# Rotary embedding on one core: the cosine and sine tables are loaded ahead of the first batch of x

## The chip, the cores and the metric

The kernel runs on one core of a Trainium2 chip. The metric is the device time of one execution in microseconds (us). Before the change the median of 3 runs was 161.33 us, the lowest 161.15 and the highest 161.42.

A core has five engines that run their own instruction streams and meet only at semaphores: TensorE (PE, matmul), VectorE (DVE), ScalarE (ACT), GpSimd (POOL) and SyncE (SP). Transfers between the chip's main memory (DRAM) and the on-chip memory are issued by an engine as an instruction and carried out by 16 DMA engines that all issuers share. In this kernel SyncE and ScalarE issue them, and each has a queue of its own in the profile: q1 is SyncE's, q10 ScalarE's.

## The reference

```python
batch, seq, dim = 16, 512, 1024          # float32, num_heads = 16
x = x.reshape(batch, seq, 16, 64)
x1, x2 = x[..., :32], x[..., 32:]
cos, sin = cos[None, :, None, :], sin[None, :, None, :]      # both (512, 32)
out = np.concatenate([x1 * cos - x2 * sin, x1 * sin + x2 * cos], axis=-1)
```

So every row of x, of 1024 elements, is cut into 16 heads of two halves, and each element becomes itself times cos, plus its partner in the other half times sin, with a minus sign for the first half. x and the output have 33.55 MB each; cos and sin have 64 KB each.

## The kernel before, in words

**Tiles.** The 512 positions of a batch are spread over 128 partitions. The first two and the last two batches are tiles of their own ("singles"): a partition holds 4 positions (R1 = 4), 16 KB of one batch, and the tile is 2 MB. The twelve batches between them are taken in pairs: a partition holds 8 positions (R2 = 8), the tile is 4 MB. That makes 10 tiles, t = 0 to 9, with 4, 4, 8, 8, 8, 8, 8, 8, 4, 4 rows; a "row" u (0 to 63) is 128 partitions by 1024 elements, and it is the unit of compute. The tiles live in a ring of 40 rows in on-chip memory (`x_sb`), and the result of a row overwrites the row.

**One row.** POOL (L257) makes t2 = partner times sin; VectorE (L293) makes t1 = x times cos in PSUM. Then they are added, in one of two ways: VectorE adds them (L304), or, in three of every eight rows (the list PE2), TensorE adds t2 on top of t1 by a matmul with the identity (L224) and ScalarE copies the sum back (L191). In one row of each pair tile VectorE makes t2 as well (L286). A store takes the tile when its last row is done.

**The tables.** cos and sin are loaded in the layout of the single tiles into `stage`, one half each. VectorE copies cos into PSUM (L264) and then waits for the PSUM banks that TensorE clears (L201). ScalarE waits for sin and makes the signed sin table of the single tiles from it (L182 and L183); POOL's first row waits for that table (L251) and then for its tile (L255). For the pair tiles, whose rows lie differently over the partitions, two pairs of matmul instructions (L208) spread both tables into PSUM with a selection matrix (`pick`, which ScalarE makes at L177), and ScalarE makes the second sin table (L186, L187). POOL asks for that one before the first row of tile 2 (L253), VectorE at the same place (L269).

**Order of the transfers.** All loads are issued by ScalarE, in the function `on_scalar`, through the helper at L153. At the start it issues six: tile 0, then cos and sin (L174), then tiles 1 to 5, which fill the ring. The other four loads wait for ring space: tiles 6, 7 and the two singles 8 and 9 are issued after the stores of the first, second and third group of eight ring rows have landed (L194). All stores are issued by SyncE in tile order (L161), each after the adds of its tile; SyncE does nothing before the first of them, and it waits for the last stores at the end (L162). The two queues are independent, so loads and stores share the DMA engines whenever both have work.

Of the kernel before, what the change touches and what calls it, by code (L numbers as in the profile page):

```python
# [6 lines left out]
def bass_split_heads_rope_kernel(  # L7
# [21 lines left out]
    R1 = seq // P  # L29
# [38 lines left out]
    with ExitStack() as stack:  # L68
        x_sb = stack.enter_context(nc.sbuf_tensor([P, RING, H, 2, HALF], fp32))
        t2_sb = stack.enter_context(nc.sbuf_tensor([P, NT2, H, 2, HALF], fp32))  # L70
        stage = stack.enter_context(nc.sbuf_tensor([P, 2, R1 * HALF], fp32))
# [11 lines left out]
        sem_cos = stack.enter_context(nc.semaphore("cos"))  # L83
        sem_sin = stack.enter_context(nc.semaphore("sin"))
# [28 lines left out]
        def in_dram(single, pairs, t):  # L113
            b, n = tiles[t]
            return single[b] if n == R1 else pairs[:, b:b + 2, :]

        def in_sbuf(t):
            b, n = tiles[t]
            k = b * R1 % RING
            return x_sb[:, k:k + n].rearrange("p n h t d -> p (n h t d)")  # L120

        def where(u):
            t, r = rows[u]
            return t, r, u % RING
# [7 lines left out]
        def wait_added(eng, u):  # L132

            if n_pe[u]:
                eng.wait_ge(sem_a, n_pe[u])
            if n_comb[u]:
                eng.wait_ge(sem_v, n_comb[u])
# [10 lines left out]
        def stores_of(k):  # L148

            return sum(b * R1 // R2 == k for b, _ in tiles)  # L150

        def load(eng, t):
            eng.dma_start(in_sbuf(t), in_dram(x1, x2, t)).then_inc(sem_in[t], 16)  # L153

        def on_sync(sp):
            for u in range(NU):
                t, r, k = where(u)
                if r == tiles[t][1] - 1:
                    wait_added(sp, u)
                    k = u // R2  # L160
                    sp.dma_start(in_dram(o1, o2, t), in_sbuf(t)).then_inc(sem_out[k] if k < EARLY else sem_rest, 16)  # L161
            sp.wait_ge(sem_rest, 16 * sum(stores_of(k) for k in range(EARLY, NU // R2)))  # L162

        def on_scalar(ae):
            later = {}
            for t, (b, n) in enumerate(tiles):
                if b * R1 + n <= RING:
                    load(ae, t)
                else:

                    later.setdefault((b * R1 - RING) // R2 * R2 + R2 - 1 + LAG, []).append(t)
                if t == 0:
                    for i, (table, sem) in enumerate(((cos, sem_cos), (sin, sem_sin))):
                        ae.dma_start(stage[:, i, :], table.rearrange("(s r) d -> s (r d)", r=R1)).then_inc(sem, 16)  # L174

            ae.wait_ge(sem_i, 2)
            ae.activation(  # L177
                pick[:], ident[:].rearrange("q (s k) -> q k s", k=2)[:, :, :, None].broadcast_to([P, 2, P // 2, 2]), COPY
            ).then_inc(sem_g, 1)
            ae.wait_ge(sem_sin, 16)  # L180
            sv = stage[:, 1, :].rearrange("s (r d) -> s r d", d=HALF)
            ae.activation(s1_sb[:, :, 0, :], sv, COPY, scale=-1.0)  # L182
            ae.activation(s1_sb[:, :, 1, :], sv, COPY).then_inc(sem_s, 1)  # L183
            ae.wait_ge(sem_t, 2)
            s2 = s2_sb[:].rearrange("p (k r) t d -> p k r t d", r=R1)
            ae.activation(s2[:, :, :, 0, :], pair_ps[:, :, 1, :, :], COPY, scale=-1.0)  # L186
            ae.activation(s2[:, :, :, 1, :], pair_ps[:, :, 1, :, :], COPY).then_inc(sem_s, 1)  # L187
            for u in range(NU):
                if PE2[u]:
                    ae.wait_ge(sem_e, n_pe[u])  # L190
                    ae.activation(xs[:, u % RING, :], t1_ps[:, u % NT1, :], COPY).then_inc(sem_a, 1)  # L191
                for t in later.get(u, ()):
                    k = (tiles[t][0] * R1 - RING) // R2
                    ae.wait_ge(sem_out[k], 16 * stores_of(k))  # L194
                    load(ae, t)
# [65 lines left out]
        def on_vector(ve):  # L261
# [49 lines left out]
            for u in range(NU + LEAD):  # L311
                if u < NU:
                    mul(u)
                if u >= LEAD and not PE2[u - LEAD]:
                    comb(u - LEAD)

        on_sync(nc.sync)
        on_scalar(nc.scalar)
        on_gpsimd(nc.gpsimd)
        on_tensor(nc.tensor)  # L320
# [34 lines left out]
```

## Time and profile before

| What | Value |
|---|---|
| median of 3 runs (lowest to highest) | 161.33 us (161.15 to 161.42) |
| the profiled execution, first to last instruction (its span) | 160.3 us |
| busy: POOL, VectorE, TensorE, ScalarE | 134.9, 130.3, 72.8, 24.4 us |
| bytes moved, mean rate over the span | 67.26 MB, 419 GB/s |
| tables landed and used: VectorE's copy of cos, ScalarE's first use of sin | 9.04 us, 9.26 us |
| POOL's first row begins | 9.85 us |
| first store issued | 20.48 us |
| last tile's first row begins on POOL | 141.02 us |
| last row's add ends on VectorE | 151.63 us |

The profile is of one execution. For that execution only the span is given; the runs are timed from outside it and the median is 1.0 us longer than the span, so a sum made on the span is carried over to the median by adding that difference. Times in the text are counted from the start of the span. A slice table divides the span into 40 parts, with the busy share of each engine in tenths. The chain of waits goes back from the last instruction to what released it, step by step. Besides these views the trace holds a record of every DMA packet: queue, start, duration and size. It doesn't say which of the 16 engines carried a packet.

### The profile page before, as it was taken

The numbers are of one execution on the slowest core, as the hardware profiler recorded it, in microseconds if no ns is written. First come the engines' busy times: TensorE is split into PE (matmuls) and PEld (weight loads), VectorE is DVE, ScalarE is ACT, GpSimd is POOL, SyncE is SP. The second block draws the span as 40 slices with busy tenths as digits, with TensorE's granted clock in tenths as the row PEclk, the third lists the DMA queues.
The fourth block names the chain that finished last, engine by engine and source line by source line (L and its number), as shares of the span: only waits on it lengthen the run. The fifth ranks groups of instructions, "written<-read, shape, count | busy, mean of one in ns | idle before, by whom it ended". The sixth has DMA issues, their size and how long they took to land.

```text
span 160.3 us, 522 instructions
## 1 busy us (share of the span) xinstructions
PE 72.8 (45%) x94; PEld 24.0 (15%) x94; DVE 130.3 (81%) x117; ACT 24.4 (15%) x27; POOL 134.9 (84%) x64
## 2 busy tenths in 40 slices
PE   6050004478357936660847105489458435850000
PEld 1020002022202211210221002022202111220000
DVE  0069998599989999996999709899889999999500
ACT  0420000203120222022012010201220402040000
POOL 1059999999999999999999999699999999289400
PEclk9955555557755587689687965555555977699555
DMA  5999999999999999999999999999999999999896
GB/s 147 409 441 474 409 450 409 425 429 429 446 429 458 417 411 466 409 433 401 450 433 425 425 409 458 409 433 433 411 429 462 441 417 401 450 441 441 376 450 294
DMA packets 3170, 67.26 MB, mean 419 GB/s; under 512 B 352, under 2 KB 608, under 8 KB 608
## 3 DMA queue, kind: packets, MB, share of 16 engines
q10 hardware_dynamic: 1728, 33.69, 49.6%
q1 hardware_dynamic: 1440, 33.56, 48.9%
q14 instruction: 2, 0.02, 0.0%
HBM read 33.69 MB, written 33.55 MB: 419 GB/s over the span
## 4 chain that ended last, share of the span: by engine, by line
DMA 60%; POOL 13%; DVE 8%; PE 7%; issue 3%; ACT 2%; ACTq 1%; DVEq 0%
DMA x_sb<-in_x_dram 41%; DMA out_dram<-x_sb 18%; POOL t_sb L257 13%; PE t_ps L224 7%; DVE t_ps L293 5%; DVE x_sb L304 3%; ACT x_sb L191 2%; ACTq L153 1%; ACTq L174 1%; DVE t_sb L286 0%; DVEq L303 0%
## 5 line engine op out<-in xcount | busy, mean ns | idle before, releaser
L257 POOL TENSOR_TENSOR t_sb<-x_sb,s_sb 128x1024 f32<-128x1024 f32 x58 | 134.2, 2346 | 14.8 <-ACT s_sb L183 8.5
L224 PE MATMUL t_ps<-t_sb,ident 128*128 128x512 f32 x84 | 68.0, 957 | 63.0 <-DVE t_ps L293 39.2
L293 DVE TENSOR_TENSOR t_ps<-x_sb,pair_ps 128x1024 f32<-128x1024 f32 x48 | 57.7, 1223 | 9.9 <-ACT x_sb L191 9.8
L304 DVE TENSOR_TENSOR x_sb<-t_ps,t_sb 128x1024 f32<-128x1024 f32 x43 | 52.4, 1218 | 2.6 <-POOL t_sb L257 2.6
L224 PEld LDWEIGHTS t_ps<-t_sb,ident 128*128 128x128 f32 x84 | 22.1, 290 | 108.9 <-DVE t_ps L293 74.6
L191 ACT ACTIVATE x_sb<-t_ps 128x1024 f32<-128x1024 f32 x21 | 21.5, 1023 | 109.9 <-PE t_ps L224 96.9
L293 DVE TENSOR_TENSOR t_ps<-x_sb,tab_ps 128x1024 f32<-128x1024 f32 x16 | 19.3, 1222 | 0.1
L286 DVE TENSOR_TENSOR t_sb<-x_sb,tab_ps 128x1024 f32<-128x1024 f32 x6 | 7.3, 1213 | 0.0
L264 DVE COPY tab_ps<-stage 128x128 f32<-128x128 f32 x1 | 0.3, 294 | 7.8 <-DMA stage<-in_cos_dram 7.8
L208 PE MATMUL pair_ps<-stage,pick 128*128 128x256 f32 x4 | 2.0, 667 | 5.4 <-DMA stage<-in_sin_dram 5.4
L201 PE MATMUL t_ps<-zero 128*128 128x512 bf16 x6 | 2.7, 627 | 1.3 <-DVE zero L262 1.3
L208 PEld LDWEIGHTS pair_ps<-stage,pick 128*128 128x128 f32 x4 | 1.2, 324 | 6.4 <-issue 6.3
L177 ACT ACT_TABLE_LOAD x1 | 1.3, 1283 | 5.5 <-issue 5.5
L201 PEld LDWEIGHTS t_ps<-zero 128*128 128x128 bf16 x6 | 0.7, 136 | 2.4 <-DVE zero L262 1.2
L262 DVE MEMSET zero<- 128x256 uint32 x1 | 0.3, 272 | 0.9 <-PEq L337 0.9
L186 ACT ACTIVATE s_sb<-pair_ps 128x256 f32<-128x256 f32 x1 | 0.4, 383 | 1.7 <-PE pair_ps L208 1.7
L182 ACT ACTIVATE s_sb<-stage 128x128 f32<-128x128 f32 x1 | 0.3, 309 | 2.1 <-DMA stage<-in_sin_dram 2.1
L235 POOL MEMSET ident<- 128x128 f32 x1 | 0.2, 204 | 0.3 <-POOLq L337 0.3
L177 ACT ACTIVATE pick<-ident 128x256 f32<-128x256 f32 x1 | 0.4, 416 | 0.0
L187 ACT ACTIVATE s_sb<-pair_ps 128x256 f32<-128x256 f32 x1 | 0.4, 379 | 0.0
L237 POOL TENSOR_SCALAR_AFFINE_SELECT ident<-ident 128x128 f32<-128x128 f32 x1 | 0.3, 292 | 0.1
L337 POOL MEMSET const-float32-0.0<- 128x1 f32 x1 | 0.1, 98 | 0.3 <-issue 0.3
(6 smaller groups left out, 1.0 us busy)
## 6 DMA issues: line engine op xcount, KB each, us to landing
x_sb<-in_x_dram ACTq DMA_DIRECT2D x6, 4096.0 KB, 38.0
out_dram<-x_sb SPq DMA_DIRECT2D x6, 4096.0 KB, 25.0
x_sb<-in_x_dram ACTq DMA_DIRECT2D x4, 2048.0 KB, 22.6
out_dram<-x_sb SPq DMA_DIRECT2D x4, 2048.0 KB, 15.2
stage<-in_cos_dram ACTq DMA_DIRECT2D x1, 64.0 KB, 7.8
stage<-in_sin_dram ACTq DMA_DIRECT2D x1, 64.0 KB, 7.5
```

The source lines that it names most:

```text
L153: eng.dma_start(in_sbuf(t), in_dram(x1, x2, t)).then_inc(sem_in[t], 16)
L174: ae.dma_start(stage[:, i, :], table.rearrange("(s r) d -> s (r d)", r=R1)).then_inc(sem, 16)
L177: ae.activation(pick[:], ident[:].rearrange("q (s k) -> q k s", k=2)[:, :, :, None].broadcast_to([P, 2, P // 2, 2]), COPY).then_inc(sem_g, 1)
L186: ae.activation(s2[:, :, :, 0, :], pair_ps[:, :, 1, :, :], COPY, scale=-1.0)
L191: ae.activation(xs[:, u % RING, :], t1_ps[:, u % NT1, :], COPY).then_inc(sem_a, 1)
L201: pe.matmul(t1_ps[:, k, b * BANK:(b + 1) * BANK], zero[:, 0:P], zero[:], start=True, stop=True).then_inc(sem_w, 1)
L208: pe.matmul(pair_ps[:, k].rearrange("p c r d -> p (c r d)"), pick[:, k].rearrange("q s b -> q (s b)"), stage[:].rearrange("q c f -> q (c f)"),
L224: ins = pe.matmul(t1_ps[:, u % NT1, b * BANK:(b + 1) * BANK], ident[:], t2[:, b * BANK:(b + 1) * BANK], start=False, stop=True, skip_group ...
L257: pl.tensor_tensor(t2_sb[:, u % NT2, :, :, :], swapped(k), over_heads(s_of(t, r)), mult).then_inc(sem_p, 1)
L286: ve.tensor_tensor(t2_sb[:, u % NT2, :, :, :], swapped(k), over_heads(v_ps), mult)
L293: ve.tensor_tensor(t1_ps[:, u % NT1, :].rearrange("p (h d) -> p h d", d=HALF), x_sb[:, k, :, :, :].rearrange("p h t d -> p (h t) d"), c_of ...
L304: ve.tensor_tensor(xs[:, k, :], t1_ps[:, u % NT1, :], t2_sb[:, u % NT2, :, :, :].rearrange("p h t d -> p (h t d)"), add,).then_inc(sem_v, 1)
```

## The change

SyncE's first act becomes the load of cos, ScalarE's first act the load of sin. The load of tile 0 follows as ScalarE's second transfer, and the loads of tiles 1 to 5 follow it directly. Destinations, sizes, semaphores and everything that waits for the tables are as before.

```diff
+        def load_table(eng, i, table, sem):
+            eng.dma_start(stage[:, i, :], table.rearrange("(s r) d -> s (r d)", r=R1)).then_inc(sem, 16)
+
         def on_sync(sp):
+            load_table(sp, 0, cos, sem_cos)
             for u in range(NU):
                 t, r, k = where(u)
                 if r == tiles[t][1] - 1:
...
         def on_scalar(ae):
+            load_table(ae, 1, sin, sem_sin)
             later = {}
             for t, (b, n) in enumerate(tiles):
                 if b * R1 + n <= RING:
...
                     later.setdefault((b * R1 - RING) // R2 * R2 + R2 - 1 + LAG, []).append(t)
-                if t == 0:
-                    for i, (table, sem) in enumerate(((cos, sem_cos), (sin, sem_sin))):
-                        ae.dma_start(stage[:, i, :], table.rearrange("(s r) d -> s (r d)", r=R1)).then_inc(sem, 16)
```

## The prediction

> **What bounds the kernel now.** I read the slice table first: it shows whether any resource is full all the time.
>
> ```profile
> span 160.3 us, 522 instructions
> ...
> PE 72.8 (45%) x94; PEld 24.0 (15%) x94; DVE 130.3 (81%) x117; ACT 24.4 (15%) x27; POOL 134.9 (84%) x64
> ...
> DMA  5999999999999999999999999999999999999896
> ...
> q10 hardware_dynamic: 1728, 33.69, 49.6%
> q1 hardware_dynamic: 1440, 33.56, 48.9%
> ```
>
> The DMA row has a 9 in nearly every slice, and the queues' packets fill 49.6 + 48.9 = 98.5% of the span. POOL is at 84%. The DMA engines are the bound, and only the first slice and the last ones have room. So I cut the edges finer (columns: stretch, length, busy PE, PEld, DVE, ACT, POOL, PE clock, DMA share, GB/s):
>
> ```profile
> 2.25:3.50 1.25, 1.25 (x5) 0.29 (x2) 0.00 (x0) 0.00 (x0) 0.00 (x0) 1.00 0.69 210
> 4.00:7.50 3.50, 0.00 (x0) 0.00 (x0) 0.00 (x0) 1.70 (x2) 0.00 (x0) 1.00 0.99 421
> 7.50:8.00 0.50, 0.00 (x0) 0.00 (x0) 0.00 (x0) 0.00 (x0) 0.00 (x0) 0.68 0.84 295
> 8.00:20.00 12.00, 2.05 (x4) 1.18 (x4) 10.35 (x10) 1.17 (x4) 10.15 (x5) 0.50 1.02 438
> 55.00:105.00 50.00, 23.91 (x32) 7.64 (x31) 42.74 (x38) 8.19 (x8) 48.22 (x22) 0.74 1.00 429
> 140.00:158.00 18.00, 2.36 (x5) 0.88 (x4) 10.55 (x10) 2.05 (x2) 9.27 (x4) 0.69 0.99 428
> ```
>
> The rate is about 430 GB/s with loads alone (8 to 20), with both (55 to 105) and with stores alone (140 to 158): the mix does not matter. Below it lie the ramp, up to 4 us, and the dip from 7.5 to 8.0, where the tables' 512-byte packets pass.
>
> Then the start and the end in order of time (start, duration, what):
>
> ```profile
> 0.81 0.37 ACTq L153 DMA_DIRECT2D x_sb<-in_x_dram  x1
> 1.21 0.46 ACTq L174 DMA_DIRECT2D stage<-in_cos_dram  x1
> 1.69 0.45 ACTq L174 DMA_DIRECT2D stage<-in_sin_dram  x1
> 2.17 3.27 ACTq L153 DMA_DIRECT2D x_sb<-in_x_dram  x5
> 9.04 0.29 DVE L264 COPY tab_ps<-stage 128x128 f32<-128x128 f32 x1 [7.84 <-DMA stage<-in_cos_dram]
> 9.26 0.31 ACT L182 ACTIVATE s_sb<-stage 128x128 f32<-128x128 f32 x1 [2.08 <-DMA stage<-in_sin_dram]
> 9.85 32.35 POOL L257 TENSOR_TENSOR t_sb<-x_sb,s_sb 128x1024 f32<-128x1024 f32 x14 [8.48 <-ACT s_sb L183]
> ...
> 135.58 16.46 SPq L161 DMA_DIRECT2D out_dram<-x_sb  x3
> 141.02 9.27 POOL L257 TENSOR_TENSOR t_sb<-x_sb,s_sb 128x1024 f32<-128x1024 f32 x4 [3.92 <-DMA x_sb<-in_x_dram]
> 150.40 1.23 DVE L304 TENSOR_TENSOR x_sb<-t_ps,t_sb 128x1024 f32<-128x1024 f32 x1 [1.08 <-POOL t_sb L257]
> ```
>
> Tile 0 lands at about 8.8 (issued at 0.81, shortest landing 8.0), but POOL starts at 9.85, because it waits for the sin table. At the end POOL waits for the last load (3.92 us idle), and the last store is issued at 151.7.
>
> Last, the packet records. Tile 0's first packet starts at 1.83, 1.0 us after its issue began. The first packet of all 16 engines can't be told apart by name, but 15 packets start between 1.83 and 2.60 and the 16th at 2.96, so a 128-row transfer reaches the engines over 1.1 us. First packets take 0.6 to 1.9 us; from 4 us on a 16 KB packet takes 0.61 us. A 512-byte packet takes 0.027 us. The last stores' landings, engine by engine, come 4.86 us after those of the store before, for 8 packets of 0.61 = 4.89: no engine pauses between the last two stores.
>
> **The change, part by part.**
>
> *Moved issues.* SyncE is ready at the same time as ScalarE (both pass their start semaphore at 0.73) and idle until 20.48, so cos costs no engine anything there. ScalarE issues sin at 0.81 and tile 0 at 0.81 + 0.37 + 0.03 = 1.21: 0.40 later. Tiles 1 to 5 are issued about 0.46 earlier (one issue of 0.46 less), which is worth nothing: their queue is full until 70 us anyway. ScalarE's own work (table load at 5.47, `pick` at 6.76) comes 0.5 earlier, hidden likewise.
>
> *Table chain.* Tables that go first land near 3 to 4 us, so cos is copied (0.29), and both sin halves are made (0.31 + 0.29) right after `pick`, by about 7.3 us. The wait for sin goes from POOL's path; what is late next is tile 0 itself. POOL gains 9.85 - 8.83 = 1.02 us, less the delay a of tile 0. The pair tables are made from about 7 instead of 9.4 and wanted near 26: no effect.
>
> *DMA stream.* Call a the delay of tile 0 on the engines. Behind tile 0 the tables no longer pass: per engine 16 x 0.027 + 2 x 0.009 = 0.45 us (bounded the other way by the per-engine landings: cos 0.25 after tile 0, sin 0.20 after cos, again 0.45). So everything from tile 1 on shifts by a - 0.45, and as the engines never idle later, so does the end.
>
> *The size of a.* No row shows tables on an empty start. Lower bound: tile 0's slow first packets (1.24 us mean for the first 15, against 0.61) are a cost of the first access that the tables would pay; then a = 0.40 - 0.63, about -0.2. If only the issue counts, a = 0.40. If a transfer's 1.1 us spread is the pace at which its packets are handed to the engines, tile 0 follows sin on the same queue by 1.1. If both queues are handed out by one source, 2.2. Between 0.40 and 1.1 I take 0.80. For 0.40 speaks that the two table issues came 0.46 apart; for 1.1 that the engine that gets its packets last sets the end, and that the issue of tile 1 took 0.66, against 0.34 for the same size as the last store (151.7), as if the hand-over were lagging already. Sum: 0.80 - 0.45 = +0.35 us.
>
> One section of the Trainium skill, "DMA: Bandwidth & Descriptors", "Bandwidth", speaks against the change: it gives 0.95 us of engine time for a 64 KB transfer (measured on another issuing path) and calls small transfers descriptor-dominated. By that the two tables would hold tile 0 back by 1.9 us and the end by 1.45, to 162.8; the trace has 0.45 for both behind other traffic, and no row at an empty start.
>
> *What the earlier start of compute does.* POOL starts 1.02 - a earlier, and so the first store. From then on loads share the engines: by queue, loads and stores move 286 and 144 GB/s from 25 to 50 us, 215 and 213 from 55 to 105, 139 and 291 from 127 to 139. One packet each in turn, of 16 or 32 KB, fits all three. Under that rule a store stream that starts d earlier ends the loads d later, and a stream that is s ahead ends them 2s earlier. With d = 1.02 - a and s = 0.45 - a the last load moves by 0.12 + a, that is 0.92 for a = 0.80, and the last store's issue with it, to 152.6. Does that set the end? The store before it leaves its first engine at about 153.85. With the 1.0 us from issue to first packet seen at the start, the last store could have begun at 152.7: 1.15 us in hand. Used are (0.12 + a) + (0.45 - a) = 0.57, whatever a is. So the earlier compute gains nothing at the end and costs nothing; should the cover go, each further us costs one.
>
> **Forecast.** 161.33 + 0.35 = 161.7 us. A difference within 0.2% (0.32 us) is about what a measurement of this kernel can't tell from no change, so this lies at that edge.
>
> **The rivals.**
> - *No change.* Only the issue counts: a = 0.40, end -0.05, 161.3. For it: the 0.46 us cadence. Against it: the 1.1 us spread.
> - *Faster.* The tables fill the ramp, where the engines move 210 instead of 430 GB/s from 2.25 to 3.5, and tile 0 comes with its first packets at full pace: a from 0.1 to -0.2, end -0.35 to -0.65, 160.8. It decides when tile 0 lands before 8.9. Against it: packets that started late (0.6 us) ended no later than early ones, which looks like waiting for packets, not like a first-access cost.
> - *Much slower.* One source hands out both queues' packets: a = 2.2, end +1.75, 163.1. The skill ("DMA: Bandwidth & Descriptors", "Queues, rings and completion order") says the two issuers have rings but no descriptor generator of their own; no row here shows it.
> - *Compute tail.* The last store starts late. Its issue-to-packet time can be at most 153.85 - 151.7 = 2.15 in the run before, or the engines had paused. With 2.15, and the last store's 6.5 us from first packet to end, it ends at 152.6 + 2.15 + 6.5 = 161.25, +0.9, 162.2. It decides from 2.15 - 0.57 = 1.6 us on. The one other row, the first store (issue 20.48, packet 23.9), had full engines before it.
>
> **How the numbers follow.** Chances: forecast 0.47 (three quarters of it beyond +0.32, the rest within), no change 0.17 (0.15 within, 0.01 on each side), faster 0.22 (0.20 beyond, 0.02 within), one source 0.07, compute tail 0.07. Slower: 0.35 + 0.01 + 0.14 = 0.50; same: 0.12 + 0.15 + 0.02 = 0.29; faster: 0.21. Range: from the middle of the faster case, 160.8, to 162.6, past the tail case; left out are the single source and the far end of faster. The forecast's own range is 161.3 to 162.0 (a from 0.40 to 1.1).
>
> **What the profile after would show.** Right: cos copied and sin used before tile 0 lands; POOL's first row released by the load of x, at 9.4 to 9.9; the dip at 7.5 to 8.0 gone; DMA row still full; last load near 141.9; end later by what tile 0 is late, less 0.45. Tile 0 landing before 8.9 or after 10.5 would prove the size of a wrong; a pause between the last two stores would prove the cover wrong; unequal shifts of start and end would prove the single-bound reading wrong.

## The result and the profile after

The changed kernel takes 161.71 us (median of 17 runs, 161.29 to 162.74), the kernel before beside it 161.33 (17 runs, 161.10 to 161.86). The ratio is 1.0025 with a 95% interval of 1.0015 to 1.0035: slower by 0.40 us, between 0.24 and 0.56. The forecast was 161.7. The number came out, but partly by luck: one term of the sum was too large, and something that the sum does not hold made up for it. A ratio here leaves out runs more than 1.5% above the fastest of their kernel: one in e4, six of twelve in e6, seven of twelve in e11 and four of the kernel before.

The profiled execution of the changed kernel spans 160.4 us, of a run of 161.79. In the 17 runs the time is always 1.42 us (1.39 to 1.46) longer than the span. The page of the kernel before shows a span of 160.3, which by this difference belongs to a run of about 161.7 and not to the median one. A second profile of the kernel before, taken for this reason (c1 below), spans 159.9 in a run of 161.32, and comparisons from here on are made with it.

The page of the changed kernel, the lines that show the bound:

```profile
span 160.4 us, 522 instructions
...
DMA  5999999999999999999999999999999999999996
...
q10 hardware_dynamic: 1584, 33.62, 49.4%
q1 hardware_dynamic: 1584, 33.62, 48.8%
```

The DMA engines are as full as before. Only one table's 144 packets have moved from ScalarE's queue (q10) to SyncE's (q1). The changed kernel in order of time, at its start and at its end (start, duration, what, idle time before it and what ended that):

```profile
0.80 0.38 SPq L156 DMA_DIRECT2D stage<-in_cos_dram  x1
0.81 0.40 ACTq L156 DMA_DIRECT2D stage<-in_sin_dram  x1
1.24 3.59 ACTq L153 DMA_DIRECT2D x_sb<-in_x_dram  x6
3.00 0.29 DVE L266 COPY tab_ps<-stage 128x128 f32<-128x128 f32 x1 [1.80 <-DMA stage<-in_cos_dram]
6.48 0.29 ACT L184 ACTIVATE s_sb<-stage 128x128 f32<-128x128 f32 x1
9.28 4.65 POOL L259 TENSOR_TENSOR t_sb<-x_sb,s_sb 128x1024 f32<-128x1024 f32 x2 [7.90 <-DMA x_sb<-in_x_dram]
...
133.46 18.62 SPq L165 DMA_DIRECT2D out_dram<-x_sb  x3
141.07 9.27 POOL L259 TENSOR_TENSOR t_sb<-x_sb,s_sb 128x1024 f32<-128x1024 f32 x4 [4.03 <-DMA x_sb<-in_x_dram]
150.44 1.22 DVE L306 TENSOR_TENSOR x_sb<-t_ps,t_sb 128x1024 f32<-128x1024 f32 x1 [1.08 <-POOL t_sb L259]
```

VectorE uses cos at 3.00, sin lands at 3.15, and POOL's first row now waits for tile 0 and not for the sin table. Both were foretold; the row's time, 9.28, lies just below the 9.4 to 9.9 that was said. Against the second profile of the kernel before:

```profile
9.69 4.65 POOL L257 TENSOR_TENSOR t_sb<-x_sb,s_sb 128x1024 f32<-128x1024 f32 x2 [8.32 <-ACT s_sb L183]
...
140.60 9.27 POOL L257 TENSOR_TENSOR t_sb<-x_sb,s_sb 128x1024 f32<-128x1024 f32 x4 [3.64 <-DMA x_sb<-in_x_dram]
149.98 1.22 DVE L304 TENSOR_TENSOR x_sb<-t_ps,t_sb 128x1024 f32<-128x1024 f32 x1 [1.00 <-POOL t_sb L257]
```

Compute starts 0.41 earlier and its last row ends 0.46 later (149.98 + 1.22 against 150.44 + 1.22). The DMA rate of the changed kernel, cut as before (stretch, length, busy PE, PEld, DVE, ACT, POOL, PE clock, DMA share, GB/s):

```profile
1.75:2.25 0.50, 0.50 (x3) 0.21 (x2) 0.00 (x0) 0.00 (x0) 0.00 (x0) 1.00 0.40 121
2.25:3.50 1.25, 1.25 (x5) 0.30 (x2) 0.29 (x1) 0.00 (x0) 0.00 (x0) 1.00 1.15 253
7.50:8.00 0.50, 0.50 (x2) 0.00 (x0) 0.00 (x0) 0.00 (x0) 0.00 (x0) 0.50 1.07 459
55.00:105.00 50.00, 25.32 (x32) 7.98 (x32) 43.56 (x39) 7.55 (x8) 49.46 (x23) 0.74 1.00 432
140.00:158.00 18.00, 1.20 (x3) 0.20 (x1) 9.42 (x8) 1.02 (x1) 9.27 (x4) 0.59 0.99 424
```

The dip at 7.5 to 8.0 is gone (459 against 295 GB/s), and the same work stands at the front: 121 GB/s from 1.75 to 2.25, where the first profile of before had 328:

```profile
1.75:2.25 0.50, 0.50 (x3) 0.20 (x2) 0.00 (x0) 0.00 (x0) 0.00 (x0) 1.00 1.74 328
```

The trace also has the time at which each of the 16 engines counts a transfer's semaphore up. They answer the question of the sum. The delay below is that of tile 0, the shift that of tile 1, both means over the engines and against c1; the last columns are the last store's landing.

| Kernel | tile 0 lands | delay | tile 1 lands | shift | last store, mean | last engine |
|---|---|---|---|---|---|---|
| before, c1 | 8.23 | | 13.53 | | 159.42 | 159.86 |
| before, first profile | 8.21 | -0.02 | 13.51 | -0.02 | 159.79 | 160.31 |
| changed | 8.75 | 0.52 | 13.64 | 0.11 | 159.60 | 160.35 |

Tile 0 is issued 0.43 later and lands 0.52 later; behind it 0.41 of that is won back. So the load stream as a whole is 0.11 late, and the mean engine ends 0.18 late, but the last engine ends 0.49 late. Between these two executions, most of what is lost beyond the start lies in how far the engines have drifted apart: the last one is 0.75 behind their mean, against 0.44 in c1. But the first profile of the kernel before has the same start as c1 and ends 0.45 later on its last engine. One execution of each kernel cannot show that the drift comes from the change.

### The profile page after: what moved, and what is told of

Read it like the earlier page. It is cut to its first block, busy times and chain, and to the rows that moved or that the text cites. A ratio compares the mean times of both kernels' runs of the same rounds, so it can differ in the third digit from the quotient of the medians.

```text
span 160.4 us, 522 instructions
## 1 busy us (share of the span) xinstructions
PE 72.3 (45%) x94; PEld 23.3 (15%) x94; DVE 130.4 (81%) x117; ACT 24.3 (15%) x27; POOL 134.8 (84%) x64
## 4 chain that ended last, share of the span: by engine, by line
DMA 60%; POOL 19%; DVE 9%; issue 4%; ACTq 1%; DVEq 0%; SPq 0%
DMA x_sb<-in_x_dram 42%; POOL t_sb L259 19%; DMA out_dram<-x_sb 19%; DVE x_sb L306 5%; DVE t_ps L295 4%; ACTq L153 1%; DVE t_sb L288 1%; ACTq L156 0%; DVEq L305 0%; SPq L137 0%
## 5 line engine op out<-in xcount | busy, mean ns | idle before, releaser
L210 PE MATMUL pair_ps<-stage,pick 128*128 128x256 f32 x4 | 1.4, 478 | 2.6 <-ACT pick L179 2.6
L210 PEld LDWEIGHTS pair_ps<-stage,pick 128*128 128x128 f32 x4 | 0.7, 189 | 3.6 <-ACT pick L179 3.5
```

What stands on the lines that cost most here:

```text
L210: pe.matmul(pair_ps[:, k].rearrange("p c r d -> p (c r d)"), pick[:, k].rearrange("q s b -> q (s b)"), stage[:].rearrange("q c f -> q (c f)"),
```

## The experiments

Ratios are to the kernel before on the same chip, with their 95% interval. Landings are means over the engines unless said otherwise, and shifts are against c1. Edits are shown against the kernel before, or against the changed kernel where the text says so; `load_table` is the helper that the change adds, and `...` marks what is left out.

**c1, the kernel before once more.** No edit.

> The kernel before, unchanged, so that its spans are seen beside its times in many runs. Of the changed kernel's 17 runs each shows its span: median 160.3 us, and the time is 1.42 us (1.39 to 1.46) longer than the span; of the kernel before only one span is known, 160.3, against a median time of 161.33. Span theory: the changed kernel loses its 0.38 us between the first and the last instruction, so the spans here have a median near 159.9 and the time is again 1.42 longer. Rim theory: the 0.38 us lie outside the span, so the spans here have a median near 160.3 and the time is 1.0 longer. Both: ratio 1.000 within 0.001.

161.28 us, ratio 0.9994 (0.9979 to 1.0008). Its spans have a median of 159.9, the changed kernel's 160.3, and the time is 1.4 longer than the span in both. So the loss lies inside the span, and the rim theory (a loss outside it) falls.

**e1, both tables ahead on ScalarE.**

```diff
         def on_scalar(ae):
+            load_table(ae, 0, cos, sem_cos)
+            load_table(ae, 1, sin, sem_sin)
             later = {}
...
-                if t == 0:
-                    for i, (table, sem) in enumerate(((cos, sem_cos), (sin, sem_sin))):
-                        ae.dma_start(stage[:, i, :], table.rearrange("(s r) d -> s (r d)", r=R1)).then_inc(sem, 16)
```

> cos and sin both ahead of tile 0, both issued by ScalarE; SyncE issues no load. Tile 0 is issued at 0.81 + 2 x 0.43 = 1.67, 0.86 later than before. Span theory (end = delay of tile 0 less the 0.45 us that the tables no longer take behind it): tile 0 lands 0.9 later, span +0.4, time 161.7 to 161.8. Rim theory with SyncE's early load as the cause: the time less the span stays as in the kernel before, so only the span counts: also +0.4, but all of it inside the span and none outside.

161.97 us, ratio 1.0044 (1.0028 to 1.0060): 0.71 later, between 0.45 and 0.97, a little above the 161.7 to 161.8 expected. Tile 0 is issued at 1.70 (0.89 later), lands 0.94 later, tile 1 lands 0.54 later. So tile 0's delay is again the issue delay plus a few hundredths, and about 0.4 of it is won back behind it.

**e2, both tables on SyncE, beside tile 0.**

```diff
         def on_sync(sp):
+            load_table(sp, 0, cos, sem_cos)
+            load_table(sp, 1, sin, sem_sin)
...
-                if t == 0:
-                    for i, (table, sem) in enumerate(((cos, sem_cos), (sin, sem_sin))):
-                        ae.dma_start(stage[:, i, :], table.rearrange("(s r) d -> s (r d)", r=R1)).then_inc(sem, 16)
```

> Tile 0 is ScalarE's first issue again (0.81); both tables are issued by SyncE at 0.8 and 1.2, beside it. Span theory: tile 0 is held up by at most the tables' 0.45 us of packets and by nothing else, which is then missing behind it: span -0.2 to +0.05, time 161.1 to 161.4. Rim theory: the same span, and 0.4 more outside it, because SyncE issues loads at the start: time 161.5 to 161.8.

161.97 us, ratio 1.0039 (1.0023 to 1.0055), in runs that scatter from 161.26 to 162.39. The time outside the span is 1.42 here too, so the rim theory falls again, but the stream sum's 161.1 to 161.4 is missed by most runs as well: tile 1 lands only 0.05 later, and the time is 0.63 longer (0.37 to 0.89). No run here explains that. The list of transfers (KB each, us from issue to landing) and the timeline of this kernel show something not foreseen:

```profile
stage<-in_cos_dram SPq DMA_DIRECT2D x1, 64.0 KB, 6.3
stage<-in_sin_dram SPq DMA_DIRECT2D x1, 64.0 KB, 10.9
```

```profile
12.79 2.35 POOL L259 TENSOR_TENSOR t_sb<-x_sb,s_sb 128x1024 f32<-128x1024 f32 x1 [11.42 <-ACT s_sb L185]
```

A 64 KB table on the other queue takes 6.3 and 10.9 us, against 2.2 and 2.3 in the changed kernel. Each engine has 8 packets of 512 bytes of cos and 8 of 16 KB of tile 0, and takes them in turn, so cos is done when tile 0 nearly is, and sin takes its turns with tile 1. POOL starts 3.1 later than in c1, and yet this execution (a run of 161.30, the second fastest of the twelve) spans 159.9 like c1: three microseconds of compute at the start cost nothing in this one.

**e3, only cos moved to SyncE.** Tile 0 stays first on ScalarE, sin stays behind it.

```diff
         def on_sync(sp):
+            load_table(sp, 0, cos, sem_cos)
...
                 if t == 0:
-                    for i, (table, sem) in enumerate(((cos, sem_cos), (sin, sem_sin))):
-                        ae.dma_start(stage[:, i, :], table.rearrange("(s r) d -> s (r d)", r=R1)).then_inc(sem, 16)
+                    load_table(ae, 1, sin, sem_sin)
```

> Only the cos half of the change: SyncE issues cos at the start, ScalarE issues tile 0 first, then sin as before. Span theory: tile 0 is delayed by at most 0.22 us (one table's packets), returned behind it: span +0.0 (-0.1 to +0.1), time 161.3. Rim theory: the same span, time less span 1.4: time 161.7.

161.51 us, ratio 1.0009 (0.9993 to 1.0026): not told apart from before. The time outside the span is 1.43.

**e4, the delay by itself.** Tile 0 later, tables where they were.

```diff
             later = {}
+            ae.wait_ge(sem_z, 1)
             for t, (b, n) in enumerate(tiles):
```

> The kernel before with one thing more: ScalarE waits for VectorE's clearing of zero (ends at 1.19) ahead of its first load, so tile 0 and all that follows on that queue is issued 0.43 later, and the tables stay behind tile 0. Stream sum (the end moves by the delay of tile 0, less what the tables no longer take behind it): nothing is returned here, so +0.43, time 161.75. If a delay of the first load is partly taken up later (by spread between the engines or by the ring), less: 161.4 to 161.6.

161.88 us, ratio 1.0031 (1.0013 to 1.0049): 0.50 later, between 0.21 and 0.79. ScalarE's first issue in its timeline:

```profile
1.23 0.38 ACTq L153 DMA_DIRECT2D x_sb<-in_x_dram  x1
...
10.12 4.66 POOL L258 TENSOR_TENSOR t_sb<-x_sb,s_sb 128x1024 f32<-128x1024 f32 x2 [8.76 <-ACT s_sb L184]
```

0.42 later issue, tile 0 and tile 1 0.38 and 0.39 later, the last store 0.48 later in the mean. A delay of the first load is paid in full, as far as the interval tells.

**e5, the tables' packets taken out.** The output is not the reference's: cos and sin are ones.

```diff
-                if t == 0:
-                    for i, (table, sem) in enumerate(((cos, sem_cos), (sin, sem_sin))):
-                        ae.dma_start(stage[:, i, :], table.rearrange("(s r) d -> s (r d)", r=R1)).then_inc(sem, 16)
...
+            ve.memset(stage[:], 1.0).then_inc(sem_cos, 1)
+            ve.wait_ge(sem_cos, 1)
...
```

> The kernel before without the two table loads: VectorE fills the staging tile with ones, so cos and sin are all ones and the output is not the reference's. Tile 0 is issued at 0.81 as before and POOL starts when it lands, 1.0 earlier than before. Stream sum: the 0.45 us of table packets per engine are gone, -0.45, time 160.9. No return (the tables' packets cost nothing where they stand): 161.3. Early compute costs (an earlier first store makes the end later by about 0.3): -0.45 + 0.3, time 161.2.

161.08 us, ratio 0.9975 (0.9958 to 0.9992): 0.40 earlier, between 0.13 and 0.68. Tile 1 lands 0.46 earlier (13.07), the last store 0.42 earlier in the mean. So the 0.45 fits: the tables' packets behind tile 0 cost the end about what they take. POOL's first row starts at 8.87:

```profile
8.87 4.66 POOL L253 TENSOR_TENSOR t_sb<-x_sb,s_sb 128x1024 f32<-128x1024 f32 x2 [7.50 <-ACT s_sb L184]
```

The line names the second sin table, which ends at the same moment; but this row waits for the first one, made by 6.4, and for tile 0, whose last engine lands at 8.7.

e4 and e5 together are the change in two halves: +0.50 and -0.40, sum +0.10, with an uncertainty of about 0.4 (0.29 and 0.28 added in squares). The change measured +0.40, which this uncertainty still covers. In the mean landings the halves are +0.48 and -0.42, sum +0.06, and the changed kernel shows +0.18.

**e6, the changed kernel with POOL held back,** to test whether an earlier first store costs something.

```diff
+            ae.wait_ge(sem_z, 1)
             ae.wait_ge(sem_t, 2)
+            for k in (4, 5):
+                ae.activation(t2_sb[:, k, 0:8].rearrange("p h t d -> p (h t d)"), zero[:], COPY)
...
                 if (t, r) == (0, 0):
-                    pl.wait_ge(sem_s, 1)
+                    pl.wait_ge(sem_s, 2)
```

> The changed kernel with POOL's first row held back: ScalarE writes two unused slots (about 0.55 us each) before the second sin table, and POOL's first row waits for that one, so it starts near 9.9 as in the kernel before, and so does the first store, while tables and tile 0 move as in the change. Early compute costs: the time goes back to 161.35. Stream sum and no return: 161.7 as with the change.

161.34 to 169.76 us in 12 runs, median 163.81, six of them above 164; ratio 1.0042 (1.0009 to 1.0074). POOL started at 10.51 and not near 9.9, so the place was missed, and the theory that early compute costs is not decided by this run. (e5 starts POOL at 8.87, and its interval, 160.7 to 161.3, holds both the 160.9 of the stream sum and the 161.2 of that theory.) The time did not go back, it grew and scattered. The theory taken up next was that the start of the store stream, relative to the load packets, decides how far the engines drift apart.

**e7, tile 0 cut in two halves of 64 partitions, one on each issuer.**

```diff
+        def load_half(eng, h):
+            p = slice(h * P // 2, (h + 1) * P // 2)
+            eng.dma_start(in_sbuf(0)[p], in_dram(x1, x2, 0)[p]).then_inc(sem_in[0], 16)
+
         def on_sync(sp):
+            load_half(sp, 1)
...
-                if b * R1 + n <= RING:
+                if t == 0:
+                    load_half(ae, 0)
+                elif b * R1 + n <= RING:
...
```

(POOL's and VectorE's waits for tile 0 then count both halves.)

> The kernel before with tile 0 cut in two: ScalarE issues partitions 0 to 63, SyncE 64 to 127, both at 0.8; the tables stay on ScalarE behind the first half. If the first packets wait for their hand-over to the engines, two issuers hand over at once, tile 0 lands up to 0.5 earlier and the end comes 0.3 to 0.5 earlier, time 160.9. If they pay a first access, no change, 161.3. If loads from SyncE at the start cost something later, as the two kernels with tables on SyncE alone suggest (+0.2 with one such load, +0.6 with two, where the stream sum is 0.0), 161.5 to 161.7.

166.85 us, ratio 1.0335 (1.0298 to 1.0371). All three expectations miss. The cut at the start of this kernel:

```profile
4.00:12.00 8.00, 0.00 (x0) 0.00 (x0) 0.00 (x0) 1.70 (x2) 0.00 (x0) 1.00 0.94 202
14.00:20.00 6.00, 1.60 (x4) 0.70 (x3) 5.44 (x6) 0.66 (x2) 5.97 (x3) 1.00 1.03 442
```

The engines are busy (0.94) and move 202 GB/s, half of what they move for 128 partitions; a 16 KB packet takes about 1.2 us and not 0.61. Tile 1 lands 4.5 later, and the last store 4.6 later in the mean. The two halves were issued at the same 0.80, but SyncE's first packet starts at 5.62 and ScalarE's at 2.17, so two issuers brought nothing forward here; whether first packets wait to be handed over can't be read from this.

**e8, e9, e10, the kernel before with nothing moved but POOL's first row,** by one, two and three ScalarE copies; the edit of e8, with `range(2)` and `range(3)` in the other two:

```diff
             ae.wait_ge(sem_sin, 16)
+            ae.wait_ge(sem_z, 1)
+            for j in range(1):
+                ae.activation(t2_sb[:, 5 - j // 2, 8 * (j % 2):8 * (j % 2) + 8].rearrange("p h t d -> p (h t d)"), zero[:], COPY)
```

> The kernel before, with no load moved: ScalarE copies 512 zeros a partition into an unused slot (about 0.53 us) ahead of the first sin table, so POOL's first row, and with it the first store, comes about 0.53 later (near 10.4). Engine-spread theory: when stores first take turns with the 32 KB load packets (1.21 us each), the place in that packet turn decides how far the DMA engines drift apart, and the last engine sets the end; half a turn is the worst place, so 161.8 or more, with widely scattered runs, as in the run with POOL held near 10.5 (161.3 to 169.8). Stream sum alone (only the start of the load stream counts): 161.35. Late compute costs what it is late: 161.9, without scatter.

> The same with two such copies: POOL's first row about 1.05 later (near 10.9), nearly one packet turn. Engine-spread theory: back at a good place, 161.4 to 161.5. Stream sum alone: 161.35. Late compute costs: 162.4.

> The same with three copies: POOL's first row about 1.6 later (near 11.4). Engine-spread theory with a turn of 1.21 (one 32 KB load packet): 0.37 into the next turn, 161.6 to 162.0; with a turn of 1.83 (a 32 KB load and a 16 KB store packet): almost back, 161.4. Stream sum alone: 161.35. Late compute costs: 162.9.

| Kernel | POOL's first row | time, us | ratio (interval) |
|---|---|---|---|
| before, c1 | 9.69 | 161.28 | 0.9994 (0.9979 to 1.0008) |
| e8 | 10.34 | 167.79 | 1.0417 (1.0395 to 1.0440) |
| e9 | 10.75 | 162.28 | 1.0068 (1.0052 to 1.0085) |
| e10 | 11.18 | 162.41 | 1.0072 (1.0049 to 1.0095) |

Holding the first row by 0.65 us costs 6.7, by 1.06 costs 1.1, by 1.49 costs 1.2. No theory had e8 in its size, and the turn theory's 161.4 to 161.5 for e9 is refuted. That late compute costs what it is late fits e9 by its size, and e10 just within its interval (0.8 to 1.5), but not as a cause: e9 issues its last store at 150.57, before c1 (151.28). The end of e8, in order of time, its DMA rate there, and then that of c1:

```profile
135.64 21.74 SPq L161 DMA_DIRECT2D out_dram<-x_sb  x3
146.37 9.26 POOL L260 TENSOR_TENSOR t_sb<-x_sb,s_sb 128x1024 f32<-128x1024 f32 x4 [6.19 <-DMA x_sb<-in_x_dram]
155.73 1.23 DVE L307 TENSOR_TENSOR x_sb<-t_ps,t_sb 128x1024 f32<-128x1024 f32 x1 [1.08 <-POOL t_sb L260]
```

```profile
150.00:155.00 5.00, 0.00 (x0) 0.00 (x0) 4.66 (x5) 0.00 (x0) 5.00 (x3) 0.50 0.93 400
155.00:160.00 5.00, 0.00 (x0) 0.00 (x0) 1.23 (x1) 0.00 (x0) 0.63 (x1) 0.50 0.54 226
```

```profile
155.00:160.00 5.00, 0.00 (x0) 0.00 (x0) 0.00 (x0) 0.00 (x0) 0.00 (x0) 0.50 0.74 318
```

Here the DMA engines run dry (226 GB/s from 155 to 160; c1 has 318 there, with its end inside the stretch), and the compute tail sets the end: POOL waits for the last load until 146.37. The landings say why. The engines finish that load at 139.59 in the mean, as in c1 (139.71), but the last one at 146.30, the next at 139.95. One DMA engine of 16 has fallen 6 us behind on its loads, and POOL waits until all 16 have counted up. Then come four rows of POOL and the last store, alone: issued at 157.0, landed at 165.7. In e9 no engine hangs back (last load: last engine 139.82); there the packets themselves took 0.8 us more per engine in sum (158.40 against 157.59 in c1), most of it between 92 and 125 us.

The packet records carry this further. The 32 KB packets have a median of 1.21 us, but some take longer, and what they take beyond the median, summed and divided by 16 engines, differs between executions: 0.56 us in c1, 0.57 in the changed kernel, 0.96 in the first profile of before, 1.21 in e9, 1.75 in e8. This difference plus the shift of tile 1 gives the shift of the last store's mean landing within 0.06 us in ten executions (before, changed, e1, e3 to e7, e9, e10). It misses e2 by 0.25, and it does not apply to e8 and e11, whose last store waits for compute. In e8, 92 of the 1536 packets take over 1.3 us, 34 in c1, and one engine is late with its stores too (the one issued at 119.3 lands at 146.51, on the next engine at 141.58). That speaks for longer packets on this engine and not for a place in the turn, but which engine carried a packet is not recorded. Why packets take longer, and why in one engine, is not shown by any run here.

**e11, the changed kernel with POOL put back behind the load stream as far as in the kernel before.**

```diff
             ae.wait_ge(sem_sin, 16)
+            ae.wait_ge(sem_z, 1)
+            for j in range(5):
+                ae.activation(t2_sb[:, 5 - j // 2, 8 * (j % 2):8 * (j % 2) + 8].rearrange("p h t d -> p (h t d)"), zero[:], COPY)
+            ae.activation(t2_sb[:, 3, 8:8 + 4].rearrange("p h t d -> p (h t d)"), zero[:, 0:256], COPY)
```

> The changed kernel with five such copies and a half one ahead of the first sin table, so that POOL's first row starts near 9.95: as far behind the load stream as in the kernel before (9.85, stream 0.1 later). Engine-spread theory: the 0.3 us that the stream sum does not explain go, 161.4 to 161.5. Stream sum alone or a cost of SyncE's early load: 161.7 as with the change.

161.35 to 169.95 us in 12 runs, median 165.53, seven of them above 164; ratio 1.0035 (1.0013 to 1.0057). POOL started at 10.19, 0.24 later than meant, so the place was missed and the test is inconclusive as such. The profiled execution, of the longest run, shows e8's picture again, with the last load at 149.10 on the last engine, 148.22 on a second one and 140.46 in the mean:

```profile
149.16 9.26 POOL L263 TENSOR_TENSOR t_sb<-x_sb,s_sb 128x1024 f32<-128x1024 f32 x4 [6.05 <-DMA x_sb<-in_x_dram]
```

So in three kernels (e6, e8, e11) a first row 0.4 to 0.7 us later against tile 1's landing than in c1 went with many runs of 164 to 170 us. In e4, e9 and e10, at about 0, 1.1 and 1.6, one run of 24 was as long (165.5, in e4), and the kernel before had four such runs (165.3 to 168.5) among 92, so it can fall there too, only rarely. None of the experiments was faster than the kernel before, except e5, which leaves the tables out.

## Why the prediction was right, and where it was not

**The bound.** Right in the main. The DMA engines are full from 4 us to the end in both kernels, and what is paid or saved in their stream at the start is paid or saved at the end: e4 (0.42 later at the start, 0.50 at the end) and e5 (0.45 of packets less, 0.40 earlier), each within 0.3. But unequal shifts of start and end were named as the sign against it, and the change has 0.11 at tile 1 and 0.40 at the end, e2 0.05 and 0.63. The sum took packets to be as long in every execution, and they are not.

**Moved issues and table chain.** Right. Tile 0 was issued 0.43 later (0.40 was said), SyncE had nothing else to do, the tables landed by 3.15, the sin table was made by 6.96 (by 7.3 was said), and POOL waited for tile 0.

**The 0.45 that the tables give back.** Right: 0.41 in the changed kernel's trace (delay 0.52, shift 0.11), 0.46 without tables.

**The size of a.** Wrong. It was 0.52 by the mean landing and 0.45 by POOL's first row (9.28 against 8.83), not 0.80. Between the bounds 0.40 and 1.1 the lower one was near. (One reading behind it was slightly off: the two table issues start 0.48 apart, at 1.21 and 1.69; 0.46 is the length of one.) The 1.1 us over which first packets start is not the pace at which a queue hands transfers over: with one transfer ahead of it tile 0 came 0.52 later, with two on the same queue (e1) 0.94, each the issue delay plus 0.05 to 0.09. The single source for both queues (2.2) is excluded by the same numbers, and so is the sum of 162.8, by which the tables would have held tile 0 back by 1.9. With a = 0.52 the sum is +0.07, the rival "no change".

**What made the number come out.** Luck: a was 0.28 too large, and about 0.3 came from where the sum has no term. The stream explains about 0.1 of the 0.40 (0.06 by the halves, 0.11 by tile 1). Tile 1 lands at 13.46 to 13.53 in the five profiles with the start of the kernel before, at 13.58 to 13.64 in the three with the start of the change, so the start alone hardly gives the 0.24 that the interval asks for. In the two executions compared, the rest is that the last engine is further behind the mean of the engines (0.75 against 0.44). That this is the cause of the median's 0.3 is not shown: two profiles of the kernel before differ as much at the end, and the halves' uncertainty would cover the 0.3. What the prediction lacked is that it treated the DMA engines as one. The end is that of the last of 16, and how far it is behind, and how long the packets take, changes from execution to execution by as much as was forecast.

**The earlier start of compute.** Half right. That it gains nothing held. That "it costs nothing" at the end, with 0.57 of 1.15 us in hand used whatever a is, was reckoned for engines in step. In the changed kernel the cover held: on the engines the last store follows the one before by 4.83 to 4.87 us, no pause. The last load, put near 141.9 (0.92 later), released POOL at 141.07, 0.47 later than in c1; by the same rule with a = 0.52 it would have been 0.64. But e8 shows the same cover gone when the first row moves by 0.65 us, through one engine's late load. The rival "compute tail" was priced at +0.9 with 0.07; its mechanism exists, its price is up to 6.7, and its trigger is another.

**The base.** The sum was put on the median with 1.0 us between span and time. It is 1.42; the profile of before was of an execution 0.4 longer than the usual one. A shift added to the median was not touched by that, but a comparison of the two pages alone (160.3 and 160.4) would have said "no change".

**Faster.** Tile 0 landed at 9.1 on its last engine, not before 8.9; the tables did not fill the ramp for nothing.

## What to carry to other kernels

In this kernel, bound by DMA from the first load to the last store, moving small loads ahead of the first large one mainly trades their packets for the issue time put in front. In a kernel like it, price both, by the issue row and by packets per engine, and expect a sum near zero. Then ask what the change does to the last of the 16 engines: a reader of the tile waits for it, and here 0.65 us in when compute and with it the stores begin cost far more than what was moved. Where two executions of one kernel differ, look at how long the packets took. And judge differences of a few tenths on the medians of many runs, with the span of each, not on one profile of each kernel.

## What the runs showed of the hardware that was not expected

- A 64 KB transfer that shares the engines with another queue's large packets advances one packet a turn: cos took 6.3 us beside 16 KB packets (e2), 5.2 in e3, and 2.2 when both queues began with a table.
- The 32 KB packets, 1.21 us in the median, took up to 2.2 (e7), and the sum of what they take beyond the median differed from 0.5 to 1.9 us per engine between executions.
- The stretch in which two loads of 64 partitions passed moved 202 GB/s, a later one with loads of 128 partitions 442 in the same execution, with the engines busy in both (0.94 and 1.03; e7).
- Holding the first row of compute by 0.65 us made the kernel before about 6.7 us longer (all six runs at 167.1 to 168.4), while 1.06 and 1.49 cost 1.1 and 1.2: in the profile of the first, one DMA engine ended its loads 6 us after the others.
